# One loop that hands out every engine's steps in the recurrence stage of a decoder block, with r, k and v kept on chip and the inverses in zeroed double buffers

## The chip, the cores and the metric

The kernel runs on one core of one Trainium2 chip. The metric is device time in microseconds (us) of one execution; lower is better. The engines spoken of are PE (TensorE, matmuls), DVE (VectorE), ACT (ScalarE), POOL (GpSimd) and SP (SyncE, which here only issues DMAs). Each engine runs its own list of instructions in the order in which they stand; an instruction whose input is not there holds up all that stands behind it on that engine.

## The reference

One decoder block on 512 tokens of width 2048, all in float32. What the stage in question computes is the RWKV-7 mixer and the pooling mixer, both fed by one input projection:

```python
h = _rmsnorm(x, norm1_g[l]) * (1.0 + sc1) + sh1
p = h @ w_in[l]
y_rwkv = _rwkv7_mixer(p[..., :N_RWKV_COLS], ...)
y_pool = _pool_mixer(p[..., N_RWKV_COLS:], ...)
mix = jnp.concatenate([y_rwkv, y_pool], axis=-1) @ w_out[l]
x = x + gt1 * mix
...
def step(S, inp):                      # inside _rwkv7_mixer, per token and head
    r_t, w_t, k_t, v_t, a_t, b_t = inp
    sa = jnp.einsum('bhvk,bhk->bhv', S, a_t)
    S = S * w_t[:, :, None, :] + sa[..., None] * b_t[:, :, None, :] + v_t[..., None] * k_t[:, :, None, :]
    y = jnp.einsum('bhvk,bhk->bhv', S, r_t)
    return S, y
```

The shifts, scales and gates (`sh1` ... `gt2`) come from `mod = silu(c) @ w_ada + b_ada`, 12288 columns: a third is made in the opening, half in the stage in question (it is used after it), the rest later. After the mixers follow the output projection, a gated MLP with a short convolution, and a last norm.

## The kernel before, in words

The program has five parts that follow one another: an opening (norm, the first third of `mod`, the first eight 128-wide tiles of the input projection, L220-L232), the recurrence stage (this document's subject, L233-L755), the output projection, the MLP up and the MLP down. Every large matmul is done as three: weights and activations are split into a high and a low float32r part, and hi*hi, hi*lo and lo*hi are summed (`mm3`, L119-L124). The split of a weight block of 128x512 is a cast on ACT (L115, `whi`) and a subtraction on DVE (L117, `wlo`).

In the recurrence stage four kinds of work run beside one another.

- **Projection.** 27 tiles of 128 output columns each: r, k and v of pairs 1 to 7, then six pooling tiles. A tile is 48 matmuls of 128x512 (L333, `mm<-ah,whi` and so on) from four weight blocks: 1296 matmuls and 108 blocks. A finished tile is shifted by a token (`shift`: one ACT and one DVE instruction, L235 and L236). For the pairs the result goes to DRAM (`spill`, `sp`, L648) and is loaded again when the pair begins (`rkv`, `v`, L387).
- **Recurrence.** The 16 heads are taken as 8 pairs of 128 channels, the 512 tokens as 8 chunks of 64. Inside a chunk the token loop becomes matrix products and the inverse of a unit triangular 64x64 matrix, 16 of them for a pair. `stage_a` builds decays, normalised keys and the scores `sb` (L378, masked on DVE at L450). The 16x16 blocks on the diagonals are then inverted: eight DMAs take them to DRAM (`dn`, L456), one brings them back in another layout (`nl`, L458), 28 small DVE instructions do the substitution (`prod` and `xyl`, L472 and L474, between L466 and L475), one DMA writes the result (`dx`, L477), eight bring it back into place (`x4w`, L479; the rest of that tile was zeroed once), and ACT copies it to a second tile (L482). This document calls the way from the first `dn` DMA to that copy the trip. `stage_b` uses the inverses (first matmul L530, `pT`), widens them to 64x64 in two levels (L530 to L564), and carries the state over the chunks (L601 and L602 in turn, six times). `post` normalises and stores the pair (L619 to L636).
- **Pools.** Running sums on DVE (L285), and two products per group on PE (L300).
- **Rows of `mod`.** 192 loads of 256 KB (`war<-ada`, L350) into three buffers, each multiplied and summed by one DVE instruction (L351).

What sets the order: `recurrence` (L679) is a loop with one clock. Each piece of recurrence work ends in a `yield` of two numbers, the time that it takes on PE and the time before its successor may run; while no piece is ready, a projection matmul is handed out and counted as 0.23, and every sixth one brings a row of `mod`. PE keeps that order word for word (`manual_schedule`). DVE, ACT, POOL and SP do not: there the tool that builds the kernel sorts the instructions by a priority (`high_priority` for the recurrence) and by its own estimates of when each is ready. `q.inverted`, 44 units after the masks, sets where L530 stands on PE.

PSUM has eight banks of 128x512: the opening uses all eight as `pf0` to `pf7` from a pool of its own, and the stage's pool (`mm`, `pa`, `pb`, `py`) is opened when all `pf` have been read (L267 is the last).

Of the kernel before, what the change touches and what calls it, by code (L numbers as in the profile page):

```python
# [16 lines left out]
P = 128  # L17
T = 512
# [10 lines left out]
NB = 10  # L29
NJ = NF // 2  # L30
# [27 lines left out]
def block_kernel(ctx, tc, a, out, stop=None, dbg=None):  # L58
# [52 lines left out]
    def split_weights(src, eng=V):  # L111
        raw = wp.tile([P, WC], F32, tag="wraw", name="wraw", bufs=4)
        nc.sync.dma_start(raw, src)
        hi = wp.tile([P, WC], F32R, tag="whi", name="whi", bufs=3)
        S.copy(hi, raw)  # L115
        lo = wp.tile([P, WC], F32R, tag="wlo", name="wlo", bufs=3)
        eng.tensor_tensor(lo, raw, hi[:, :].bitcast(F32), op=ALU.subtract)  # L117
        return hi, lo
# [7 lines left out]
    def project(ps, src, acts, start=True, stop=True, engs=(V,)):  # L126

        n = len(acts)
        for k0 in range(0, n, WC // P):
            wh, wl = split_weights(src[:, k0 * P : k0 * P + WC], engs[k0 // 4 % len(engs)])  # L130
# [45 lines left out]
    first = {}  # L176
    p0ctx = ExitStack()
    p0 = p0ctx.enter_context(tc.tile_pool(name="p0", bufs=1))
    if True:
# [24 lines left out]
        ps0ctx = ExitStack()  # L204
        ps0 = ps0ctx.enter_context(tc.tile_pool(name="ps0", bufs=1, space=PSUM))
        pf = [ps0.tile([P, T], F32, tag=f"pf{i}", name=f"pf{i}") for i in range(8)]
        H = []
        for k in range(KT):
# [14 lines left out]
            for i0 in range(0, 8, WC // P):  # L223
                wh, wl = split_weights(a["win0"][k, :, i0 * P : i0 * P + WC])
                for ii in range(WC // P):
                    sl = slice(ii * P, (ii + 1) * P)
                    mm3(pf[i0 + ii], wh[:, sl], wl[:, sl], *H[k], start=k == 0, stop=k == KT - 1)
        p0ctx.close()


        actx = ExitStack()
        ra = actx.enter_context(tc.tile_pool(name="ra", bufs=1))  # L232
        if True:  # L233
            def shift(ps, m, dst):
                S.activation(dst, ps, AF.Copy, scale=drv[:, m : m + 1])  # L235
                V.scalar_tensor_tensor(dst[:, 1:T], ps[:, 0 : T - 1], col("mu", m), dst[:, 1:T],  # L236
                                       op0=ALU.mult, op1=ALU.add)

            def ring(name):
                return ring16(name)[:, 16:]  # L240

            def ring16(name):
                return ra.tile([P, 16 + T], F32, tag="ring", name=name, bufs=7)

            xwa = ra.tile([P, T], F32, tag="xwa", name="xwa")
            shift(pf[0], 24, xwa)
            S.activation(xwa[0:64, :], xwa[0:64, :], AF.Tanh)
            xg1 = ra.tile([P, T], F32, tag="xg1", name="xg1")
            shift(pf[1], 25, xg1)
            S.activation(xg1, xg1, AF.Sigmoid)  # L250
            xg2 = ra.tile([P, T], F32, tag="xg2", name="xg2")
            shift(pf[2], 26, xg2)
            S.activation(xg2, xg2, AF.Sigmoid)

            def vtile(name):
                return ra.tile([P, T], F32, tag="v", name=name, bufs=2)

            rkv0 = []
            for i, m in ((3, 0), (4, 8), (5, 16)):
                t = vtile("v") if i == 5 else ring("rkv")  # L260
                shift(pf[i], m, t)
                rkv0.append(t)

            upad = [ring16("upad") for i in range(2)]
            for i in range(2):
                V.memset(upad[i][:, 0:16], 0.0)
                S.copy(upad[i][:, 16:], pf[6 + i])  # L267
            ps0ctx.close()

    def load_pw(gi):  # L270
        t = ra.tile([P, T], F32, tag="war", name="pw", bufs=3)
        pw = t.rearrange("p (i d) -> p i d", i=2)
        nc.sync.dma_start(pw, a["poolw"][gi, :, :, :])
        return pw

    def pool_front(gi, upad):
        win = WINS[gi]
        zs = []
        for i in range(2):
            cur = upad[i]  # L280
            lo = 1
# [1060 lines left out]
```

## Time and profile before

| | us |
|---|---|
| median of 3 runs (2345.34 to 2349.33) | 2347.96 |
| the profiled execution, its own time | 2349.0 |
| its span, first to last instruction | 2347.1 |
| recurrence stage: end of the opening's last matmul to the first matmul of the output projection | 156.0 to 761.05 |

A group's row gives line, engine, operation, output and inputs, shapes and count, then busy time and the mean of one, then the engine's idle time just before these instructions and what ended it. "PE" is a matmul, "PEld" its weight load, "SPq" the issue of a DMA on SP's queue; a DMA lands some time after its issue. A row of a window gives busy us with the number of instructions for each engine, the granted PE clock (1.00 is full speed), the share of time in which the DMA engines worked, and GB/s. Ends of matmuls are modelled, so the distance from start to start is the better measure of what one costs in a stream.

### The profile page before, as it was taken

The page shows a single profiled execution, that of the slowest core. Times are in us where ns is not written, and L with a number is a line of the kernel's source. Part 1 is how long each engine was busy: PE and PEld are TensorE (multiplying, and loading weights), DVE is VectorE, ACT ScalarE, POOL GpSimd, SP SyncE. Part 2 cuts the span into 40 slices and gives each one's busy share as a digit, 9 for nine tenths or more (in the row PEclk, how much of TensorE's full clock was granted, in tenths as well). Part 3 has the DMA queues.
Part 4 walks back from the last instruction along what each step waited for, and adds up shares of the span by engine and source line. Part 5 has one row for each costly group of instructions (what it writes and reads, how often), then busy time and mean ns, then how long its engine had stood idle before and what let it go on. Part 6 is the DMA issues. An engine that isn't in the chain of part 4 may idle for free.

```text
span 2347.1 us, 42629 instructions
## 1 busy us (share of the span) xinstructions
PE 2206.0 (94%) x17090; PEld 1958.5 (83%) x17090; DVE 1611.8 (69%) x2543; ACT 1006.5 (43%) x1416; POOL 126.1 (5%) x183
## 2 busy tenths in 40 slices
PE   4778798898899999999999999999999999999997
PEld 3656566666677799999999999999999888888897
DVE  7977786877665366788888877777777645353454
ACT  3243333333333346655555555555555422233353
POOL 0000000000000010111010100000000000110000
PEclk9999899999999999999999999999999999999998
DMA  9966665666533766698888877777776667663464
GB/s 353 339 221 187 210 198 168 202 201 186 151 77 93 251 187 184 204 271 235 250 225 248 234 200 201 199 199 197 200 197 196 221 222 268 226 211 112 124 189 155
DMA packets 200218, 480.77 MB, mean 205 GB/s; under 512 B 46481, under 2 KB 53201, under 8 KB 191825
## 3 DMA queue, kind: packets, MB, share of 16 engines
q1 hardware_dynamic: 180098, 410.91, 53.7%
q0 software_dynamic: 18864, 66.07, 13.7%
q8 instruction: 134, 2.20, 0.4%
q10 hardware_dynamic: 1056, 1.05, 0.1%
q14 instruction: 66, 0.54, 0.1%
HBM read 440.45 MB, written 37.49 MB: 204 GB/s over the span
## 4 chain that ended last, share of the span: by engine, by line
PE 67%; DVE 12%; issue 11%; DMA 8%; ACT 2%; SPq 1%; POOL 0%; DVEq 0%; POOLq 0%; ACTq 0%
PE b L124 18%; PE b L122 18%; PE b L123 18%; PE mm L333 6%; DMA war<-ada 6%; DVE jk L214 3%; DVE war L351 2%; DVE wlo L117 1%; DMA wrow<-wup 1%; PE pa L300 1%; DVE sacc L199 0%; DVE al L151 0%; PE pb L570 0%; ACT ah L150 0%; DMA cq<-cact 0%
## 5 line engine op out<-in xcount | busy, mean ns | idle before, releaser
L124 PE MATMUL b<-t,ulo 128*128 128x256 f32 x1408 | 397.2, 282 | 0.0
L122 PE MATMUL b<-t,uhi 128*128 128x256 f32 x1408 | 396.8, 282 | 0.0
L123 PE MATMUL b<-t,uhi 128*128 128x256 f32 x1408 | 396.7, 282 | 0.0
L115 ACT CAST whi<-wraw 128x512 fp32r<-128x512 f32 x236 | 145.4, 618 | 381.9 <-PE mm L333 222.9
L124 PE MATMUL b<-act,ulo 128*128 128x512 f32 (+1 forms) x880 | 308.0, 350 | 0.0
L123 PE MATMUL b<-act,uhi 128*128 128x512 f32 (+1 forms) x880 | 307.8, 350 | 0.0
L122 PE MATMUL b<-act,uhi 128*128 128x512 f32 (+1 forms) x880 | 307.7, 350 | 0.0
L122 PE MATMUL b<-y,uhi 128*128 128x256 f32 x1056 | 298.1, 282 | 2.1 <-ACT uhi L930 2.1
L124 PE MATMUL b<-y,ulo 128*128 128x256 f32 x1056 | 297.8, 282 | 0.4 <-DVE ulo L932 0.4
L123 PE MATMUL b<-y,uhi 128*128 128x256 f32 x1056 | 297.9, 282 | 0.0
L932 DVE TENSOR_TENSOR ulo<-wd,uhi 128x1024 fp32r<-128x1024 f32 (+1 forms) x120 | 136.2, 1135 | 215.6 <-ACT uhi L930 210.8
L122 PEld LDWEIGHTS b<-t,uhi 128*128 128x128 f32 x1408 | 266.9, 190 | 0.0
L124 PEld LDWEIGHTS b<-t,ulo 128*128 128x128 f32 x1408 | 266.9, 190 | 0.0
L123 PEld LDWEIGHTS b<-t,uhi 128*128 128x128 f32 x1408 | 266.8, 190 | 0.0
L930 ACT CAST uhi<-wquart 128x1024 fp32r<-128x1024 f32 x156 | 163.8, 1050 | 203.8 <-PE b L123 177.5
L930 ACT CAST uhi<-wd 128x1024 fp32r<-128x1024 f32 (+1 forms) x120 | 117.3, 978 | 291.1 <-PE b L123 290.0
L932 DVE TENSOR_TENSOR ulo<-wquart,uhi 128x1024 fp32r<-128x1024 f32 x156 | 190.9, 1224 | 71.9 <-ACT uhi L930 71.9
L117 DVE TENSOR_TENSOR wlo<-wraw,whi 128x512 fp32r<-128x512 f32 x236 | 161.2, 686 | 82.3 <-ACT whi L115 81.5
L930 ACT CAST uhi<-r 128x1024 fp32r<-128x1024 f32 x132 | 138.6, 1050 | 162.8 <-PE b L123 159.2
L932 DVE TENSOR_TENSOR ulo<-r,uhi 128x1024 fp32r<-128x1024 f32 x132 | 161.2, 1222 | 61.8 <-ACT uhi L930 61.7
L122 PEld LDWEIGHTS b<-y,uhi 128*128 128x128 f32 x1056 | 200.2, 190 | 2.5 <-ACT uhi L930 2.5
L124 PEld LDWEIGHTS b<-y,ulo 128*128 128x128 f32 x1056 | 200.1, 190 | 0.6 <-DVE ulo L932 0.6
(302 smaller groups left out, 4455.7 us busy)
## 6 DMA issues: line engine op xcount, KB each, us to landing
wquart<-wup SPq DMA_DIRECT2D x176, 512.0 KB, 4.8
wa<-ada SPq DMA_DIRECT2D x48, 1024.0 KB, 6.9
war<-ada SPq DMA_DIRECT2D x192, 256.0 KB, 3.6
wd<-wdn SPq DMA_DIRECT2D x80, 512.0 KB, 4.0
wraw<-win SPq DMA_DIRECT2D x140, 256.0 KB, 4.2
wraw<-wout SPq DMA_DIRECT2D x96, 256.0 KB, 3.6
wquart<-wup POOLq DMA_DIRECT2D x44, 512.0 KB, 7.3
r<-wup SPq DMA_DIRECT2D x44, 512.0 KB, 4.5
```

Of the source, the lines that this page charges most:

```text
L115: S.copy(hi, raw)
L117: eng.tensor_tensor(lo, raw, hi[:, :].bitcast(F32), op=ALU.subtract)
L122: PE.matmul(ps, wh, xh, start=start, stop=False, skip_group_check=more)
L123: PE.matmul(ps, wh, xl, start=False, stop=False, skip_group_check=more)
L124: return PE.matmul(ps, wl, xh, start=False, stop=stop, skip_group_check=more)
L214: V.scalar_tensor_tensor(jk, wa, 1.0, cb, op0=ALU.mult, op1=ALU.mult, accum_out=mod[:, j : j + 1])
L300: PE.matmul(ps, pw[:, i, d * P : (d + 1) * P], zs[i], start=i == 0, stop=i == 1)
L333: PE.matmul(ps, w[:, sl], x, start=k == 0 and i == 0, stop=k == KT - 1 and i == 2)
L351: V.scalar_tensor_tensor(wa, wa, 1.0, cq[0], op0=ALU.mult, op1=ALU.mult, accum_out=modq[:, kq, j : j + 1])
L930: S.copy(hi[:, 0:n], src)
L932: lo_of[0] = V.tensor_tensor(lo[:, 0:n], src, hi[:, 0:n].bitcast(F32), op=ALU.subtract)
```

## The change

What it does, by parts:

- **One loop for all engines.** Every step of every chain of work is a generator that yields an engine ("P", "V", "S", "Q" for SP, "-" for a mere condition), the time that the step holds it, and the time (or a function that gives it) before which it cannot run. `run` keeps a clock per engine, takes the step that can start earliest, lets one of better priority go ahead if it starts little later, and then emits it. The order of PE, DVE, ACT, POOL and SP is that of emission (`manual_schedule()` without a list of engines). Priorities: opening and evictions 0, `stage_b` 1, `stage_a` and `post` 2, `stage_k` (the part of `stage_a` that the inverses do not need) 3, weight blocks 0 to 4 by how near PE is to needing them, pools 5, projection matmuls 6, rows of `mod` 7.
- **r, k, v on chip.** `evict` shifts a tile into one of three `rk` or two `v` buffers, which `stage_a` reads; the 21 stores to DRAM and 21 loads are gone.
- **Inverses.** `x4` is two whole tiles, zeroed by POOL for every pair, into which the `dx` DMAs write; the ACT copy L482 is gone. `gd`, `sg` and two `fdec` tiles are zeroed once by POOL, where DVE wrote `sg`'s and `fdec`'s edges for every pair.
- **Rows of `mod`.** Five buffers in place of three, four loads ahead, each row due 460/192 units after the one before.
- **PSUM.** The opening uses the stage's own banks, and a bank is free when its own tile has been read.
- **Weights.** The first two blocks of the stage are loaded before the opening's pool is closed, later ones two blocks ahead.
- **Small ones.** Several tiles have one buffer instead of two, or share one (`sq`, `inv`; `y`, `sqy`, `rs`); a pool's result overwrites its input by way of a 16-wide `edge` tile, one more small DVE copy each; the gate product of `post` stands earlier on PE.

```diff
+NA = 4
+WARB = 5
+NTILE = 27
+PF0 = 5.5
+SPAN = 460.0
+ADAB = 0.72
...
-        ps0ctx = ExitStack()
-        ps0 = ps0ctx.enter_context(tc.tile_pool(name="ps0", bufs=1, space=PSUM))
-        pf = [ps0.tile([P, T], F32, tag=f"pf{i}", name=f"pf{i}") for i in range(8)]
+        psctx = ExitStack()
+        psa = psctx.enter_context(tc.tile_pool(name="psa", bufs=1, space=PSUM))
+        pf = [psa.tile([P, T], F32, tag=t, name="pf") for t in ("mm0", "mm1", "pa0", "pa1")]
+        for t in ("pb", "py"):
+            two = psa.tile([P, 2, T], F32, tag=t, name="pf")
+            pf += [two[:, 0, :], two[:, 1, :]]
...
+    LAT = {"P": 0.3, "V": 0.2, "S": 0.2, "Q": 0.0}
...
+    def run():
+
+        while chains:
+            best = {}
+            for c in chains:
+                eng, busy, after = c[2]
+                t = after() if callable(after) else after
+                if t is None:
+                    continue
+                t = max(t, free_at.get(eng, 0.0))
+                best.setdefault(eng, []).append((t, c[0]() if callable(c[0]) else c[0], busy, c))
+            pick = None
+            for eng, ops in best.items():
+                op = min(ops, key=lambda o: o[:2])
+                late = [o for o in ops if o[1] < op[1] and o[0] < op[0] + min(0.3, 0.5 * op[2])]
+                if late:
+                    op = min(late, key=lambda o: o[1])
+                if pick is None or op[:2] < pick[:2]:
+                    pick = op
+            t, _, busy, c = pick
+            eng = c[2][0]
+            if eng in free_at:
+                free_at[eng] = t + busy
+                t += busy + LAT[eng]
+            try:
+                c[2] = c[1].send(t)
+            except StopIteration:
+                chains.remove(c)
...
+    def weights():
+
+        land = {0: 0.5, 1: 1.0}
+        for i in range(4 * NTILE):
+            wnext[0] = i
+            if i + 2 < 4 * NTILE and i + 2 not in land:
+                t = yield "Q", 0.35, 0.0
+                load_block(i + 2)
+                land[i + 2] = t + 3.8
+            t = yield "S", 0.58, (lambda i=i: land[i] if i <= cur[0] + 2 else None)
+            raw = blocks.pop(0)
+            hi = wp.tile([P, WC], F32R, tag="whi", name="whi", bufs=3)
+            S.copy(hi, raw)
+            t = yield "V", 0.63, t
...
+    def evict(ti, ps, tag, t):
+        if ti < 21:
+            p, i = ti // 3 + 1, ti % 3
+            q = qs[p]
+            dst = vtile("v") if i == 2 else rktile("rk")
+            t = yield "S", 0.6, t
+            shift1(ps, 8 * i + p, dst)
+            t = yield "V", 0.65, t
+            shift2(ps, 8 * i + p, dst)
+            mm.give(tag, t)
...
+    def ada_rows():
+        n_all = 48 * NA
+        step = SPAN / n_all
...
+        for n in range(n_all):
+            kq, j = divmod(n, 48)
+            t = yield "V", ADAB, max(land[n], tcq, 3.0 + n * step)
+            wa = was.pop(0)
+            V.scalar_tensor_tensor(wa, wa, 1.0, cqs[kq], op0=ALU.mult, op1=ALU.mult, accum_out=modq[:, kq, j : j + 1])
...
+            if n + WARB - 1 < n_all:
+                tq = yield "Q", 0.35, 0.0
+                load_ada(n + WARB - 1)
+                land[n + WARB - 1] = tq + 4.5
...
-        x4 = q.x4 = ra.tile([P, 8, 2, 64], F32, tag="x4c", name="x4")
-        S.copy(x4, x4w)
-        q.inverted = clock[0] + 44.0
-        yield 1.35, 6.0
...
+        x4 = q.x4 = ra.tile([P, 8, 2, 64], F32, tag="x4", name="x4", bufs=2)
+        G.memset(x4, 0.0)
...
+            t = yield "Q", 0.33, t
+            nc.sync.dma_start(x4[16 * b : 16 * b + 16, :, :, 16 * (b % 4) : 16 * (b % 4) + 16],
+                              dx[8 * b : 8 * b + 8, :, :, :].rearrange("s w i j -> i s w j"))
+        q.inverted = t + 2.4
...
+    with tc.manual_schedule():
+        for prio, gen in ((0, opening()), (1, all_b()), (2, all_a()), (weights_prio, weights()), (6, projection()), (7, ada_rows())):
+            spawn(prio, gen)
+        run()
```

Every later stage keeps its instructions, on DVE, ACT and POOL in the same order as before; what moves lies in the recurrence stage. Three places show how. In the rows below a line number is that of the kernel the row belongs to: L550 after is L351 before (a row of `mod`), L416 is L117 (`wlo`), L638 is L450 (the masks on the scores), L654 is L466 and L666 is L475 (first and last step of the substitution), L661 and L663 are L472 and L474.

On DVE before, the fifth pair's masks and its substitution:

```order
L351 SCALAR_TENSOR_TENSOR war,modq<-war,cq 128x512 x2
L573 COPY rw<-pb 128x512
L351 SCALAR_TENSOR_TENSOR war,modq<-war,cq 128x512
L450 TENSOR_TENSOR sb<-pa,masks 128x4x128 x2
...
L466 TENSOR_TENSOR xyl<-nl,lanei 64x256
L602 SCALAR_TENSOR_TENSOR rw<-pb,fdec,rw 128x64
L472 TENSOR_TENSOR prod<-xyl,nl 64x14
L117 TENSOR_TENSOR wlo<-wraw,whi 128x512
L474 TENSOR_TENSOR xyl<-xyl,prod 64x14
L351 SCALAR_TENSOR_TENSOR war,modq<-war,cq 128x512
L472 TENSOR_TENSOR prod<-xyl,nl 64x26
```

On DVE after, the same pair:

```order
L686 TENSOR_TENSOR kt<-rk,em 128x512
L884 TENSOR_TENSOR y<-y,bv 128x512
L638 TENSOR_TENSOR sb<-pa,masks 128x4x128 x2
L726 TENSOR_TENSOR sk<-pb,masks 128x1024
...
L550 SCALAR_TENSOR_TENSOR war,modq<-war,cq 128x512
L654 TENSOR_TENSOR xyl<-nl,lanei 64x256
L661 TENSOR_TENSOR prod<-xyl,nl 64x14
L663 TENSOR_TENSOR xyl<-xyl,prod 64x14
L661 TENSOR_TENSOR prod<-xyl,nl 64x26
```

Before, rows of `mod` stand ahead of the masks and other work stands between nearly every two steps of the substitution; after, no row of `mod` stands near the masks, and all 28 steps from L654 to L666 stand one behind the other (in the second pair one other instruction is among them).

On SP after, the fifth pair's trip and what is queued between its DMAs (`x` is the tile that the inverses go to):

```order
L647 DMA dn_4153<-sb 16x8x16 x8
L889 DMA mixd_103<-y 128x512
L119 DMA wraw<-win 128x512
L532 DMA war<-ada 128x512
L119 DMA wraw<-win 128x512
L532 DMA war<-ada 128x512
L651 DMA nl<-dn_4153 64x256
...
L669 DMA dx_4364<-xyl 64x512
L353 DMA lw<-lora 128x128
L119 DMA wraw<-win 128x512 x2
L532 DMA war<-ada 128x512 x2
L673 DMA x_4151<-dx_4364 16x16x16 x8
```

Weight blocks and rows of `mod` now stand at fixed places between the trip's DMAs; the stores and loads of `sp` that stood there before are gone. On PE the first matmul that needs the inverses (L771, before L530) stands behind 80 projection matmuls counted from the end of that pair's scores in the first pair, 54 in the second, 88, 72, 87, 72, 80 and 87 in the others, with recurrence work of its own and of the neighbouring pair among them.

More of the change, by code (lines that the diff above doesn't have):

```diff
@@ L227, in block_kernel @@
                     mm3(pf[i0 + ii], wh[:, sl], wl[:, sl], *H[k], start=k == 0, stop=k == KT - 1)
+        for i in range(2):
+            load_block(i)
         p0ctx.close()
[L231 to L268, printed above, removed]
@@ L537, in stage_b @@
[L537 removed]
+        pa.give(tag, t)
+        t = yield "P", 1.9, max(t, tpb)
         pX = btile()
@@ L734, in block_kernel, with all_a, all_b @@
[L734 to L740 removed]
+    def all_a():
+        for p in range(NP):
+            yield from stage_a(p, qs[p])
+    def all_b():
+        for p in range(NP):
+            yield from stage_b(p, qs[p])
+    G.memset(gd, 0.0)
+    G.memset(sg, 0.0)
```

697 lines of the change are left out of this document (410 added, 287 removed).

## The prediction

> **What bounds the kernel now.** I read the page first, for the stage that the change touches, then windows, the waits, and the timeline at the longest waits. Of the page, four rows of the span in 40 slices (58.7 us each) and the chain of waits:
>
> ```profile
> PE   4778798898899999999999999999999999999997
> DVE  7977786877665366788888877777777645353454
> PEclk9999899999999999999999999999999999999998
> DMA  9966665666533766698888877777776667663464
> PE 67%; DVE 12%; issue 11%; DMA 8%; ACT 2%; SPq 1%; POOL 0%; DVEq 0%; POOLq 0%; ACTq 0%
> ```
>
> From the 14th slice on PE works nine tenths of the time or more: those parts are bound by PE, and none of them changes. The recurrence stage is slices 3 to 13, where PE has gaps and DVE is at 6 to 8 tenths. In windows (opening's end, stage with rows of `mod`, stage without them, whole stage):
>
> ```profile
> 156.00:163.09 7.09, 0.04 (x2) 0.00 (x1) 4.48 (x11) 7.00 (x12) 0.00 (x0) 0.76 0.32 110
> 163.09:650.00 486.91, 427.06 (x4251) 319.74 (x4252) 362.58 (x959) 172.52 (x265) 0.00 (x0) 0.94 0.62 187
> 650.00:761.00 111.00, 110.05 (x1231) 84.40 (x1230) 61.98 (x139) 32.83 (x54) 0.00 (x0) 1.00 0.31 86
> 156.00:761.05 605.05, 537.19 (x5481) 404.16 (x5481) 429.05 (x1107) 212.37 (x332) 0.00 (x0) 0.95 0.56 168
> ```
>
> The stage takes 605.05 us. PE is idle for 67.9 of them, and its clock is 0.95; at 650, when the last row of `mod` is done, idle time and low clock both end. So the stage is bound by PE, which is held up while the rows of `mod` run. Who holds it up, in the waits of PE:
>
> ```profile
> PE pb L563 <- DVE Tm L560: 15.4, 4, 6.5
> PE pb L601 <- DVE rw L602: 9.6, 10, 1.7
> PE mm L333 <- DVE wlo L117: 8.1, 3, 4.7
> PE pa L426 <- ACT sq L395: 8.0, 1, 8.0
> PE mm L333 <- ACT upad L267: 7.1, 1, 7.1
> ```
>
> And why DVE is late (group of L351, two waits, two rows of the timeline):
>
> ```profile
> L351 DVE SCALAR_TENSOR_TENSOR war<-war,cq 128x512 f32<-128x512 f32 x192 | 129.8, 686 | 84.0 <-DMA war<-ada 76.7 <-DMA cq<-cact 6.7
> DVE wlo L117 <- ACT whi L115: 18.3, 19, 2.2
> DVE rw L573 <- ACT rw L573: 15.7, 6, 4.3
> 543.18 0.69 DVE L351 SCALAR_TENSOR_TENSOR war<-war,cq 128x512 f32<-128x512 f32 x1 [3.68 <-DMA war<-ada]
> 543.79 1.28 DVE L450 TENSOR_TENSOR sb<-pa,masks 128x512 f32<-128x512 f32 x2
> ```
>
> DVE stands idle 84.0 us ahead of rows of `mod` whose load has not landed, and what PE needs (here the masks L450, at other places `Tm` L560) is queued behind them.
>
> **How much work PE has.** Between the first use of the inverses of the last two pairs lies nearly one pair's work without waits; the window once for all of PE, once for L333 alone, then the pace of L333 (13 issues, 12 distances) and one pool product:
>
> ```profile
> 650.45:704.70 54.25, 53.30 (x639) 40.66 (x638) 33.21 (x86) 15.91 (x26) 0.00 (x0) 1.00 0.31 78
> 650.45:704.70 54.25, 32.57 (x117) 1.00 0.31 78
> 645.29 0.39 PE L333 MATMUL mm<-al,whi 128*128 128x512 f32 x1
> ...
> 648.01 0.39 PE L333 MATMUL mm<-al,whi 128*128 128x512 f32 x1
> 698.12 3.59 PE L300 MATMUL pa<-z,pw 128*128 128x512 f32 x8
> ```
>
> The distance is 2.72 / 12 = 0.227. Off 54.25 go 117 x 0.227 = 26.5, the idle 0.95 and the pool's 3.4: 23.4 for the pair; its L401, L402 and L426 fell outside. They are six passes 512 wide, 2.6 at the pool's 3.4 / 8 each, or 1.7 if L401 and L402, which use half of the rows each, run side by side; I take 2.2. That is 25.6 a pair. The stage: 1296 x 0.227 = 294, 8 x 25.6 = 205, three pool products 10: **509 us**. Busy time by clock says the same: 537.19 x 0.95 = 510.
>
> **The change part by part.**
>
> *PSUM banks and early weights.* The first projection matmul waits 7.1 us for L267, the reader of the last opening bank. After, it needs only the bank of the first tile, which is read while the opening's last matmuls run, and a weight block that is loaded by then. Gain between 5 and 7.1; it is inside the 605 - 509.
>
> *Rows of `mod`.* 192 stay. With five buffers a load is issued four rows ahead; a row comes every 509/192 = 2.65 us, so it has 10.6 us to land, against
>
> ```profile
> DMA to landing us min/median/max: 2.4/3.6/6.5
> ```
>
> So the 84.0 of idle DVE ahead of them goes, unless SP is held up. DVE's work, 429 us, has 530 to fit in.
>
> *The trip.* Here a new wait may take the place of the old. Before, L530 stands so late in PE's order that it hardly waits. After, the order leaves fixed cover. From the end of a pair's scores to L771 PE has 54 to 88 projection matmuls and recurrence work; in the fifth pair that is 87 x 0.227 = 19.7 and second scores, four transposes, L692, L750, L758 and L762, an estimated quarter of the pair's 25.6, 6.3: 26.0 us, and, worked out alike, 26 to 27 in all others but the first (80 matmuls, a pool product and more: 29). What must fit in, from the fifth pair (rows of `mod` running) and the last (done), first `dn`, L466, L475, then `x4w`, L482:
>
> ```profile
> 470.45 4.45 SPq L456 DMA_DIRECT2D dn<-sb  x8
> 479.92 0.42 DVE L466 TENSOR_TENSOR xyl<-nl,lanei 64x256 f32<-64x256 f32 x1
> 499.30 0.38 DVE L475 COPY xyl<-xyl 64x256 f32<-64x256 f32 x1
> 509.26 1.05 ACT L482 COPY x<-x4w 128x1024 f32<-128x1024 f32 x1 [1.90 <-DMA x4w<-dx]
> ...
> 662.23 1.29 DVE L450 TENSOR_TENSOR sb<-pa,masks 128x512 f32<-128x512 f32 x2 [2.84 <-PE pa L378]
> 663.55 4.54 SPq L456 DMA_DIRECT2D dn<-sb  x8
> 672.08 0.41 DVE L466 TENSOR_TENSOR xyl<-nl,lanei 64x256 f32<-64x256 f32 x1
> 677.98 0.21 DVE L472 TENSOR_TENSOR prod<-xyl,nl 64x56 f32<-64x56 f32 x1
> 678.22 0.21 DVE L474 TENSOR_TENSOR xyl<-xyl,prod 64x56 f32<-64x56 f32 x1
> 682.72 0.37 DVE L475 COPY xyl<-xyl 64x256 f32<-64x256 f32 x1
> 686.00 3.77 SPq L479 DMA_DIRECT2D x4w<-dx  x8
> 692.69 1.05 ACT L482 COPY x<-x4w 128x1024 f32<-128x1024 f32 x1
> ```
>
> The trip took 38.8 us in the fifth pair and 29.1 in the last; the substitution alone 19.4 and 10.6. Unbroken, its 28 steps take at most 0.24 each (677.98 to 678.22) and L466 0.41: 7.1. The rest was 9.5 + 10.0 in the fifth pair and 8.5 + 10.0 in the last. So the trip becomes 25.6 to 26.6; the copy of 1.05 after it is gone. The masks ahead of it take 1.29 and a start of some 0.2. Need 27.1 to 28.1, cover 26.0: PE waits 1.1 to 2.1 in seven pairs, nothing in the first. I take 1.5: **10.5 us**; ends 0 (the DMAs may land before ACT was free to look) and 15.
>
> *The clock after such waits.* The same product warm, after 2.17 and after 4.24 us of waiting:
>
> ```profile
> 665.09 1.15 PE L563 MATMUL pb<-x,Tm 64*64 64x64 f32 x32
> 531.49 1.82 PE L563 MATMUL pb<-x,Tm 64*64 64x64 f32 x32 [2.17 <-DVE Tm L560]
> 272.90 1.97 PE L563 MATMUL pb<-x,Tm 64*64 64x64 f32 x32 [4.24 <-DVE Tm L560]
> ```
>
> A wait of two microseconds already costs 0.7 to 0.8 on the next product. Seven waits at half of it: **3 us**, ends 0 and 6. [...]
>
> *Handovers inside `stage_b`.* The 9.6 and 15.4 us of waits at L601 and L563 came with DVE's queue; the steps that follow one another are now spaced by projection matmuls. Some remain, since rows of `mod` still stand between steps of DVE (three between L793 and L798 in the fifth pair). Ends 0 and 25 (all that these two lines show); I take **8**, nearer to zero as in the stretch from 650.
>
> *r, k, v on chip.* 42 DMAs of 256 KB go, 11 MB of the stage's 605 us x 168 GB/s = 102 MB; the DMA engines work 0.56 of the time, so nothing is gained by that alone, and if the cover fails nothing is lost. Two shift instructions per tile stay. The price is that a new tile waits for its buffer's last reader, with ACT's weight casts queued behind it; in the order those readers stand ahead of the shift on every engine: 0.
>
> *SP.* The eight `x4w` issues wait for `dx` to land; behind them stand weight blocks and rows of `mod`, loaded two and four ahead. Hidden by those; if not, a block late costs what L117 cost PE before, 8.1 in all.
>
> *POOL and small DVE edits.* Eight more memsets on an engine that the four windows show idle; one 0.15 us copy more for each pool tile, some memsets fewer: 0, under the other terms' error.
>
> *After the stage* the order on DVE, ACT and POOL is unchanged and PE has work without gaps, so the gain carries to the end.
>
> **Sum.** 509 + 10.5 + 3 + 8 = 530.5 in place of 605.05: 74.5 saved. The profiled execution took 2349.0, 1.0 over the median: 2274.5, and against the median **2273**.
>
> **The rivals.**
>
> *Better than that:* no waits and all of PE's work at full clock, 509: 96 saved, 2252. For it: 650 to 761 ran almost so. Against: the cover of 26.0 is about equal to the shortest trip.
>
> *VectorE becomes the bound.* 429.05 of work, and if it still waits as before, 84.0 + 18.3 + 15.7: 547 us, 58 saved, 2290. For it: 81% of the new stage is its work, in a fixed order. Against: five buffers.
>
> *The trip shortens by half only,* say to 33, because SP, now in a fixed order, issues its seventeen DMAs late. Need 34.5, cover 26: 8.5 x 8 = 68, and 6 for the clock: 591, 14 saved, 2334.
>
> *Slower:* the trip stays at 38.8 (DMAs land late beside denser loads). PE's cover is fixed, so it waits 38.8 + 1.5 - 26 = 14.3 in eight pairs, 114, with 6 for the clock and 8 of handovers: 637, 32 more, 2380. It decides from a trip of about 35 on, where 8 waits of 10.5 with those 14 eat the 96. Against: more than half of the trip's length was interrupted substitution, and that is settled by the order.
>
> *The change doesn't do what it says:* PE's order was already full and the time stays. Against: 67.9 idle and 0.95 clock.
>
> **How the numbers follow.** My forecast 0.60; better 0.06; VectorE 0.12; half a trip 0.12; slower 0.08; no change 0.02. Faster by over 0.2% (4.7 us, about what a measurement of this kernel tells from nothing) 0.90, within 0.02, slower 0.08. The range runs from 2248 (some below the better case, if a pair's work is nearer 25) to 2330, the edge of the half trip; it leaves out the slower case and part of that one.
>
> **What would show it.** After: the stage from 156 to about 687; PE idle about 20 in it, clock at 0.98 or above; L771 waiting for `x` some 10 us in all and L796 and L844 little; no wait of 84 at rows of `mod`; from first `dn` to L771 about 26. A clock still at 0.95, or L771 above 50, would make the prediction wrong.

## The result, and the profile after

| | before | after |
|---|---|---|
| median, us | 2347.49 (2345.34 to 2349.33) | 2307.67 (2304.52 to 2314.75) |
| the profiled execution | 2349.0 | 2314.75 |
| first projection matmul to the first of the output projection | 163.1 to 761.05 | 155.2 to 721.75 |

The ratio is 0.9835, with a 95% interval of 0.9809 to 0.9860: 39.8 us faster by the medians, where 74.5 were forecast. Sign and range held; the size was about half. The profiled execution of the changed kernel is the slowest of its four, which comes up again below.

The stage in one row of the windows for each kernel, before and after, from the first to the last projection matmul (PE busy, PE weight loads, DVE, ACT, POOL, then granted clock, DMA share, GB/s):

```profile
163.10:760.40 597.30, 536.50 (x5478) 403.61 (x5479) 424.56 (x1097) 205.34 (x319) 0.00 (x0) 0.95 0.57 168
155.20:721.10 565.90, 533.05 (x5479) 401.94 (x5478) 441.77 (x1100) 204.14 (x321) 5.72 (x6) 0.97 0.55 160
```

After the change it is 565.9 us, 533.05 busy and so 32.85 idle. To see what the clock takes, I cut the stage into 23 equal slices and sum busy time x (1 - clock): 15.5 us. What is left, 517.5, is PE's work at full clock. By the same accounting the stage before is 597.3 = 60.8 idle + 23.3 clock + 513.3 work. So 27.9 of idle and 7.8 of clock went, the opening's wait of 7 went, and 4.2 of busy time came on top.

The waits of the changed kernel in the stage (total us, times, longest):

```profile
DVE war L550 <- DMA war<-ada: 22.8, 21, 4.4
...
PE pa L771 <- DMA x<-dx: 12.8, 9, 2.1
...
DVE Tm L774 <- PE pa L771: 10.9, 4, 3.8
...
PE mm L440 <- DVE wlo L416: 7.8, 3, 3.6
DVE xyl L654 <- DMA nl<-dn: 7.3, 4, 3.3
```

(L771 is the first product that uses the inverses, L774 the masking of its result on VectorE, L781 the two products that need that; L440 is a projection matmul, L416 makes its `wlo`.) VectorE's wait for rows of `mod` to land fell from 76.7 (the 84.0 of before hold 6.7 for `cq` too) to 22.8 but did not go. PE's longest item is L771, as forecast. One of these, in the fourth pair, on PE's timeline:

```profile
388.08 0.39 PE L440 MATMUL mm<-ah,wlo 128*128 128x512 f32 x1
390.60 0.29 PE L771 MATMUL pa<-x,sb 64*64 64x64 f32 x2 [2.13 <-DMA x<-dx]
392.07 1.94 PE L771 MATMUL pa<-x,sb 64*64 64x64 f32 x30 [1.17 <-DMA x<-dx]
393.94 0.79 PE L440 MATMUL mm<-ah,whi 128*128 128x512 f32 x1
394.53 0.63 PE L440 MATMUL mm<-al,whi 128*128 128x512 f32 x1
...
396.37 1.97 PE L781 MATMUL pb<-Tm,x 64*64 64x64 f32 x32
398.13 1.17 PE L781 MATMUL pb<-x,Tm 64*64 64x64 f32 x32
```

PE waits for the first `x` DMA, does two matmuls, waits for the others, and then everything takes nearly twice its time until about 398: the projection matmuls stand 0.43 apart at 394.5 to 395.8 where 0.227 is the full clock, the first product of L781 takes 1.97 and the second 1.17. That is how 3.3 us of waiting cost seven. The same with the granted clock, at another wait:

```profile
211.00:213.00 2.00, 0.04 (x1) 0.00 (x0) 1.95 (x6) 0.00 (x0) 0.00 (x0) 1.00 0.93 317
213.00:213.50 0.50, 0.41 (x14) 0.41 (x16) 0.50 (x2) 0.00 (x0) 0.00 (x0) 1.00 0.80 209
213.50:217.00 3.50, 3.50 (x60) 3.23 (x57) 2.37 (x4) 1.67 (x3) 0.00 (x0) 0.56 0.39 120
217.50:221.00 3.50, 3.50 (x42) 2.40 (x41) 2.55 (x6) 1.26 (x2) 0.00 (x0) 1.00 0.45 123
```

Two idle microseconds at full clock, half a microsecond of work, and then a stretch of about 3.5 us at half. In windows of half a microsecond the stage has eight such stretches, six of about 3.5 and two of 7 us, each behind a wait or a close pair of waits that make 1.6 to 3.6 us: five behind L771, one behind L781 (the rows above), two behind L440.

One of the two at L440, on VectorE and then on PE:

```profile
445.83 0.42 DVE L654 TENSOR_TENSOR xyl<-nl,lanei 64x256 f32<-64x256 f32 x1 [1.35 <-DMA nl<-dn]
...
452.64 0.37 DVE L666 COPY xyl<-xyl 64x256 f32<-64x256 f32 x1
452.94 1.88 DVE L416 TENSOR_TENSOR wlo<-wraw,whi 128x512 fp32r<-128x512 f32 x3
```

```profile
453.67 0.79 PE L440 MATMUL mm<-ah,wlo 128*128 128x512 f32 x1 [3.15 <-DVE wlo L416]
```

Three `wlo` stand behind the unbroken substitution, which itself had waited for `nl`.

### The profile page after: what moved, and what is told of

Read it like the earlier page. It is cut to its first block, busy times and chain, and to the rows that moved or that the text cites. A ratio compares the mean times of both kernels' runs of the same rounds, so it can differ in the third digit from the quotient of the medians.

```text
span 2313.0 us, 42595 instructions
## 1 busy us (share of the span) xinstructions
PE 2205.9 (95%) x17090; PEld 1959.5 (85%) x17090; DVE 1625.4 (70%) x2535; ACT 998.9 (43%) x1406; POOL 133.3 (6%) x193
## 4 chain that ended last, share of the span: by engine, by line
PE 84%; DVE 7%; DMA 4%; ACT 2%; issue 1%; SPq 0%; DVEq 0%; ACTq 0%
PE b L133 21%; PE b L131 21%; PE b L132 21%; PE mm L440 10%; DVE jk L231 3%; DMA war<-ada 2%; DMA wrow<-wup 1%; PE pb L781 1%; DMA nl<-dn 1%; PE pb L804 1%; PE pa L504 1%; DVE prod L661 0%; DVE xyl L663 0%; DVE sacc L213 0%; PE pa L738 0%
## 5 line engine op out<-in xcount | busy, mean ns | idle before, releaser
L1110 ACT CAST uhi<-wquart 128x1024 fp32r<-128x1024 f32 x156 | 163.8, 1050 | 204.1 <-PE b L132 175.8
L1110 ACT CAST uhi<-wd 128x1024 fp32r<-128x1024 f32 (+1 forms) x120 | 117.4, 978 | 291.8 <-PE b L132 291.6
L1110 ACT CAST uhi<-r 128x1024 fp32r<-128x1024 f32 x132 | 138.6, 1050 | 163.0 <-PE b L132 161.5
L131 PEld LDWEIGHTS b<-y,uhi 128*128 128x128 f32 x1056 | 200.3, 190 | 5.2 <-ACT uhi L1110 5.2
L132 PEld LDWEIGHTS b<-y,uhi 128*128 128x128 f32 x1056 | 199.9, 189 | 0.0
L440 PE MATMUL mm<-ah,wlo 128*128 128x512 f32 x432 | 181.7, 421 | 8.0 <-DVE wlo L416 7.8
```

What stands on the lines that cost most here:

```text
L131: PE.matmul(ps, wh, xh, start=start, stop=False, skip_group_check=more)
L132: PE.matmul(ps, wh, xl, start=False, stop=False, skip_group_check=more)
L440: PE.matmul(ps, w[:, sl], x, start=first, stop=k == KT - 1 and i == 2)
L1110: S.copy(hi[:, 0:n], src)
```

## The experiments

All runs are edits of the changed kernel. The table gives the stage from first to last projection matmul of each profiled execution, split as above, and the ratio to the kernel before on the same chip. The experiments ran on four chips, so they are best compared by their ratios.

| run | stage | idle | clock | ratio (95%) |
|---|---|---|---|---|
| the changed kernel | 565.9 | 32.9 | 15.5 | 0.9835 (0.9809 to 0.9860) |
| the same again | 562.7 | 32.0 | 13.9 | 0.9823 (0.9797 to 0.9849) |
| e1 inverses later | 550.9 | 29.6 | 3.3 | 0.9797 (0.9773 to 0.9821) |
| e2 no rows | 529.3 | 12.6 | 0 | 0.9689 (0.9669 to 0.9710) |
| e3 no trip | 524.6 | 9.5 | 0 | 0.9666 (0.9646 to 0.9687) |
| e4 three buffers | 559.4 | 32.3 | 7.6 | 0.9870 (0.9854 to 0.9886) |
| e5 rows on POOL | 570.0 | 36.2 | 18.2 | 0.9857 (0.9830 to 0.9885) |
| e6 trip priced | 519.7 | 6.0 | 0 | 0.9785 (0.9756 to 0.9814) |
| e7 rows later | 552.3 | 24.5 | 10.7 | 0.9838 (0.9812 to 0.9865) |
| e8 both | 521.2 | 6.8 | 0 | 0.9905 (0.9880 to 0.9931) |
| e9 all priced | 533.7 | 15.3 | 0 | 0.9775 (0.9755 to 0.9795) |
| e10 rows sooner | 540.1 | 23.1 | 0 | 0.9765 (0.9748 to 0.9783) |
| e11 rows spread | 533.6 | 15.6 | 0 | 0.9754 (0.9737 to 0.9770) |

PE's work at full clock is 514 to 520 in all of them: what differs is idle time, clock, and what happens behind the stage.

**e1: only L771 later.**

```diff
-        q.inverted = t + 2.4
+        q.inverted = t + 6.4
```

> The changed kernel with one number altered: q.inverted is 6.4 in place of 2.4 units after the last of the x4 DMAs, so L771 is handed out four units later on PE and projection matmuls stand in the gap. Theory (short waits and the clock behind them): the changed kernel waits 12.8 us at L771 in nine places, and nearly every stretch with a clock of 0.93 or less lies right behind one of them; by busy time x (1 - clock) those stretches lose 15.5 us. With L771 later both go: the stage falls from 567 to about 543 us and the time from 2307.7 to about 2285. Rival (VectorE sets the pace, and L771 is only where it shows): the wait comes back at L781, L796, L804 or at a wlo, the stage gains less than 5 us: 2303 to 2308. Second rival (the clock falls anyway): only the 12.8 us go: 2295.

Measured 2301.07. L771's wait went, and a wait at the next step took its place:

```profile
PE pb L781 <- DVE Tm L774: 17.4, 8, 4.0
```

The longest, on VectorE and then on PE:

```profile
582.12 0.69 DVE L550 SCALAR_TENSOR_TENSOR war<-war,cq 128x512 f32<-128x512 f32 x1 [4.71 <-DMA war<-ada]
...
584.75 0.69 DVE L774 TENSOR_TENSOR Tm<-pa,mlev 128x512 f32<-128x512 f32 x1
```

```profile
585.49 1.50 PE L781 MATMUL pb<-Tm,x 64*64 64x64 f32 x32 [4.02 <-DVE Tm L774]
```

`Tm`, the 0.69 us step between two products of PE, stands on VectorE behind a row of `mod` that had not landed. So the first rival was right on where the wait went. It was wrong that nothing would be gained: idle time is nearly the same (29.6 for 32.9), and yet the profiled stage is 15 us shorter, because the clock takes 3.3 in place of 15.5. (The medians are only 6.6 us apart and the intervals of the ratios overlap, so the gain in time is not clear of the noise.) Here the clock is nearly all that differs. Why is less plain, since e1 has waits as long. This one, of 2.21 us at L781, left the clock alone:

```profile
261.50:264.00 2.50, 0.43 (x14) 0.43 (x16) 2.49 (x6) 0.28 (x1) 0.00 (x0) 1.00 1.05 387
264.00:267.50 3.50, 3.50 (x66) 3.12 (x61) 3.16 (x9) 0.00 (x0) 0.00 (x0) 1.00 0.97 318
```

Behind e1's longest wait, the 4.02 us above, the first product of L781 took 1.50 us; behind the 2.21 us it took 1.15.

Windows set at the falls and rises of the clock show the stretches more sharply. In the profiled execution of the changed kernel they start at 213.95, 258.32, 333.42, 391.44, 452.88, 524.56, 589.41 and 650.85; six last 3.41 us and two, at 391.44 and 452.88, 6.83, all at 0.50. The first of them:

```profile
213.95:217.36 3.41, 3.41 (x45) 3.10 (x42) 2.27 (x5) 1.67 (x3) 0.00 (x0) 0.50 0.27 74
```

PE had waited 2.04 us (from 211.04) ahead of this one, and 1.64 us (at L771, from 255.39) ahead of the second; e1's 2.21 us is longer than either and left the clock at 1.00. So the length of one wait does not decide by itself whether half clock follows, and the runs do not show what does. Ends of matmuls are modelled, so these lengths are not sharp.

**e2 and e3: one of two loads taken away.** Both keep every other instruction in its place. e2 emits no loads and products of rows of `mod` (one memset on POOL zeroes the sums in their place); e3 emits nothing of the trip, from the `dn` DMAs to the `x4` DMAs, so `x4` stays zero.

```diff
-            load_ada(n)
...
-            V.scalar_tensor_tensor(wa, wa, 1.0, cqs[kq], op0=ALU.mult, op1=ALU.mult, accum_out=modq[:, kq, j : j + 1])
...
-                load_ada(n + WARB - 1)
```

and for e3

```diff
-            nc.sync.dma_start(dn[8 * b : 8 * b + 8, :, :].rearrange("s i j -> i s j"),
...
-            V.tensor_tensor(pv, xyl[:, 1, 0:s, s : s + 1].to_broadcast([64, s, n]),
...
-            nc.sync.dma_start(x4[16 * b : 16 * b + 16, :, :, 16 * (b % 4) : 16 * (b % 4) + 16],
```

> The changed kernel with the 192 rows of mod left out of the stage: neither their loads (L532) nor their products (L550) are emitted, the sums are zeroed instead; every other instruction keeps its place, since the steps are still counted in the order. So 128 us of VectorE's 442 us of work, 50 MB of DMA and the 22.8 us of waits at L550 go. Theory (short waits of PE and the clock): these waits reach PE only through a late nl or wlo, so idle falls from 33 to about 20 us and the cold stretches by a third: stage about 550, time about 2290. Rival (VectorE sets the pace): the stage goes to PE's own 518 us, time about 2260. Second rival (rows are wholly beside the path): within 4 us of 2307.7.

> The changed kernel with the trip left out: no dn, nl, dx and x DMAs and no substitution; x4 keeps POOL's zeros, so the inverses are missing from the result; every other instruction keeps its place, the steps being still counted in the order. L771 can then wait only for nt and the zeros. Theory: the 12.8 us at L771, the two waits of 3.6 and 3.2 us at L440 behind the substitution, and the cold stretches behind them (most of 15.5 us) go: stage about 535, time about 2277; PE's busy time at full clock stays at 518. Rival (the missing gain is PE's own work, sized at 509, or other handovers): only the 20 us of waits go, the clock stays at 0.97: 2288 or more. What the stage still takes over 518 is the price of all handovers that are not the trip's.

Measured 2275.37 and 2269.62. The stage of each:

```profile
154.50:683.80 529.30, 516.71 (x5479) 391.16 (x5477) 326.31 (x712) 204.65 (x321) 5.71 (x6) 1.00 0.30 76
```

```profile
156.70:681.30 524.60, 515.13 (x5479) 390.31 (x5478) 393.12 (x860) 203.99 (x320) 5.71 (x6) 1.00 0.55 166
```

Of 48.4 us of idle and clock together 12.6 and 9.5 are left, and the stages are 36.6 and 41.3 shorter. The two gains add up to more than the 48.4, so it is the two loads together that cost: the trip nearly fits under PE's cover when no rows are loaded beside it, and rows cost little when no trip runs (VectorE waits 6.9 for them in e3, 22.8 in the changed kernel). In e2 the trip is shorter though nothing of it was edited: from the first `dn` to the end of the last `x4` issue 22.1 to 25.5 us, 24.4 to 27.3 with rows, and L771 waits 2.0. The theory's 550 and 2290 for e2 were far off, and the rival's 518 and 2260 too low; e3 gained more than its theory's 535 and 2277. Rows reach PE through more than `nl` and `wlo`, namely through the trip's length and through `Tm`.

**e4: three buffers.**

```diff
-WARB = 5
+WARB = 3
```

> The changed kernel with three buffers for the rows of mod, as before the change, and so loads two ahead in place of four. By the forecast the five buffers took away the 84 us that VectorE waited for rows. Theory: with two loads ahead and 5.8 us from issue to landing, rows that stand in groups on VectorE wait again, some 40 to 80 us in all, and VectorE's later steps reach PE late: stage 580 to 600, time 2320 to 2340. Rival (the fixed order, not the buffers, took the waits away, since the rows are due at fixed times 2.4 units apart): waits at L550 stay under 40 us and the time within 5 us of 2307.7.

Measured 2318.28, below the theory's range and 10.6 above the rival's 2307.7, so neither held as to the time. The idle time of VectorE ahead of the rows:

```profile
  DMA war<-ada: 45.5, 48
```

Of the 76.7 us of before, the change with three buffers takes away 31.2 and the two more buffers another 22.7. The loss isn't in the stage (559.4): the last row stands at 751.3 in place of 713.9, in the output projection, and from the last projection matmul to the end of the span it takes 1605.1 in place of 1591.9.

**e5: rows on another queue.**

```diff
-        nc.sync.dma_start(t, a["ada2"][n // 48, n % 48, :, :])
+        nc.gpsimd.dma_start(t, a["ada2"][n // 48, n % 48, :, :])
```

> The changed kernel with the 192 loads of rows of mod (L532) issued by POOL in place of SP; nothing else moves. Leaving the rows out gave 2275, leaving the trip out 2270, the changed kernel 2308: it is the two together that cost. Theory (SP's queue): the trip's DMAs that wait for data hold up the row loads behind them, and the row loads take issue time between the trip's DMAs. On two queues both go: waits at L550 fall from 22.8 to under 10 us, the first x4 issue comes 2.4 us after dx in place of 3.0 to 4.5, L771 waits under 5 us, time about 2285. Rival (the DMA engines are shared: the trip's small packets land late beside 256 KB loads, whatever the queue): from dx to the first x4 stays at 3 us or more, L771 still waits 10 us or more, 2300 to 2312. Third (POOL is slow at issuing): rows land later than now, waits at L550 over 40 us, slower than 2315.

Measured 2313.51: no gain. From the groups of DMA issues (count, KB each, median us to landing) of the changed kernel and of e5, and then PE's wait at L771 and VectorE's for rows in e5:

```profile
x<-dx SPq DMA_DIRECT2D x64, 16.0 KB, 2.8
```

```profile
x<-dx SPq DMA_DIRECT2D x64, 16.0 KB, 4.7
```

```profile
PE pa L771 <- DMA x<-dx: 17.9, 8, 4.4
```

```profile
DVE war L550 <- DMA war<-ada: 9.6, 13, 1.6
```

The queue did hold things up: rows wait 9.6 in place of 22.8, and from the `dx` issue to the first `x4` issue it is 2.3 us in seven pairs (2.9 to 4.5 in seven pairs of the changed kernel). But the `x4` DMAs land in 4.7 us in place of 2.8, and L771 waits longer. So the theory is wrong as to the time. The first rival (shared DMA engines) comes nearest (L771 waits over 10 us, and the time is 1.5 above its range), though its sign that the `x4` issues stay late did not come: freed of the queue, the small DMAs land later beside the rows. Whether that is the sharing of the DMA engines or something in POOL's way of issuing, the run doesn't tell.

**e6, e7, e8: the loop's prices.** The loop places steps by the times it is told. e6 tells it the trip's true ones (in the order of the lines: `dn`, `nl`, a step of the substitution, `x4`), e7 a longer landing of rows, e8 both.

```diff
-            tn = yield "Q", 0.33, tn
+            tn = yield "Q", 0.45, tn
-        t = yield "V", 0.4, t + 3.6
+        t = yield "V", 0.42, t + 5.0
-            t = yield "V", 0.36, t
+            t = yield "V", 0.46, t
-            t = yield "Q", 0.33, t
+            t = yield "Q", 0.6, t
```

and the row's landing:

```diff
-                land[n + WARB - 1] = tq + 4.5
+                land[n + WARB - 1] = tq + 8.0
```

> The changed kernel with the trip's steps priced in the loop as the trace has them: a dn issue 0.45 (was 0.33), nl 5.0 after its issue (3.6), a step of the substitution 0.46 (0.36), an x4 issue 0.6 (0.33). The order then has L771 about 6 units later, and Tm, the wlo behind the substitution and the row loads on SP stand where they come out in truth. Theory: unlike the run that only moved L771 (2301, the wait came back at L781 for Tm), the steps behind move with it: L771 and L781 together wait under 10 us, no wlo wait over 1 us, cold under 5 us, time about 2292. Rival (row loads late on SP still hold Tm): L781 waits 15 us again, 2298 to 2303.

> The changed kernel with the landing of a row of mod priced at 8.0 units after its issue in place of 4.5 (the trace has 5.8 from issue to landing as the median, and SP holds some issues up), so its product stands later on VectorE. Theory (rows that have not landed stand ahead of the steps PE waits for): waits at L550 fall from 22.8 to about 8 us; L771 still waits about 10 us, since its own DMAs are as late: 2300. Rival (waits at L550 are not what holds PE): within 4 us of 2308.

> Both tables of prices together: the trip's as in the run with the trip priced, the row's landing at 8.0. Theory: the two waits that feed each other (L771 on the trip, Tm behind rows that have not landed) go together, PE idle under 18 us, cold under 3 us, stage about 540, time about 2283. Rival (moving both later only pushes the pair's later steps into the end of the stage, where no projection is left): 2298 or more.

Measured 2296.22, 2310.11 and 2324.44. e6's stage, then its largest wait of PE, and SP's row behind that:

```profile
155.00:674.70 519.70, 513.74 (x5478) 390.53 (x5477) 419.65 (x1035) 201.53 (x316) 5.72 (x6) 1.00 0.54 158
```

```profile
PE pb L131 <- ACT whi L124: 26.9, 1, 26.9
```

```profile
669.62 25.59 SPq L532 DMA_DIRECT2D war<-ada  x28
```

The stage is shorter than the prediction's 530.5: 519.7 with 6.0 idle and no clock lost. So PE's waits in the stage came from the prices. But it is not the same work in less time, because the rows are not through: 26 of the 192 products stand behind the stage's last projection matmul, 28 loads are issued in one run from 669.6 on, as PE finishes the projection, and the output projection's first weights stand behind them. By the profiles 46 us were gained in the stage and 26.9 paid back at once; by the ratios the kernel gained about 12 us over the changed kernel, and the two intervals overlap a little. e8 shows it larger:

```profile
PE pb L131 <- ACT whi L124: 53.4, 2, 37.1
```

```profile
690.39 38.49 SPq L532 DMA_DIRECT2D war<-ada  x43
```

I had not expected this in e8 at all: as I read it, pricing a row's landing at 8 with five buffers slows the rows, and 56 products are left when the projection ends; no run takes that apart. e8's rival had 2298 or more, but for another reason. e7 falls to the same (a wait of 9.8 there) and its L771 still waits 11.4: no gain, as its rival said, though its waits at L550 did fall, to 3.7. (The expectations of e4 and e7 give 5.8 us from a row's issue to its landing; the trace of the changed kernel has 4.2 as the median.)

**e9, e10, the changed kernel again: rows priced as measured.**

On top of e6, with 3.3 in place of 3.85 in e10:

```diff
-ADAB = 0.72
+ADAB = 0.62
...
-                land[n + WARB - 1] = tq + 4.5
+                land[n + WARB - 1] = tq + 3.85
```

> The kernel with the trip priced, and the rows of mod priced as measured as well: a product 0.62 (was 0.72), a landing 4.2 after its issue, so 3.85 after the step (was 4.5). With the trip priced alone PE's projection ended 519.7 us after its first matmul with 6.0 us idle and no cold stretch, but 31 rows were left over, SP issued 28 of them in a run from 669.6 to 695.3, and PE then waited 26.9 us for the first weights of the output projection, which stand behind them. Theory: in the loop's own clock the last row moves from 531 to 510 and the last projection tile from 516 to 511, so that wait falls to under 3 us; the stage takes 520 to 530 us and the time is 2268 to 2278, ahead of both kernels. Rival (rows packed more densely bring the waits back): idle of 20 us or more in the stage, 2290 or more.

> The same with a landing priced at 3.3 after the step, less than measured: rows stand a little sooner on VectorE, last row at 507 by the loop's clock. Theory: the wait ahead of the output projection is gone as well, but rows that have not landed stand ahead of the steps PE waits for: waits at L550 back to 20 us or more, L781 or L771 waiting 5 to 10 us; 2275 to 2285. Rival (with the trip priced there is slack enough on VectorE): equal to the run before it within 4 us.

> The changed kernel unaltered, beside the two others on the same chip: 2304 to 2315, ratio 0.981 to 0.986. If its executions differ again by 10 us, the clock in them differs too: a shorter one has a higher mean clock, since a wait of about two microseconds at L771 sometimes brings a cold stretch of 3.5 us and sometimes not.

Measured 2295.41, 2292.71 and 2305.33. The wait ahead of the output projection in e9, and in e10:

```profile
PE pb L131 <- ACT whi L124: 13.4, 1, 13.4
```

```profile
PE pb L131 <- ACT whi L124: 4.4, 1, 4.4
```

It shrinks as rows come sooner, and the stage grows: 519.7 in e6, 533.7, 540.1. Stage and wait together are 546.6, 547.1 and 544.5: time moved from one place to the other. Both theories missed, since they counted the wait as gone for nothing. Both rivals had the time (2290 or more for e9; within 4 us of e9 for e10) but not the reason: e9 idles 15.3 in the stage, not 20, and e10 idles 7.8 more than e9, so VectorE had no slack left. The changed kernel again ran from 2300.58 to 2311.69, at a mean clock of 0.990 and 0.985.

**e11: the last 16 rows between the blocks of the output projection.**

On top of e9; `more_rows` is the product of L550 with the next load issued by POOL:

```diff
+NROW = 176
...
-        for n in range(n_all):
+        for n in range(NROW):
...
         last = out_block(f, 0)
+        more_rows(NROW + 2 * f, NROW + 2 * f + 2)
```

> The kernel with the trip and the rows priced as measured, with the last 16 of the 192 rows of mod taken out of the stage's loop and handed out two at a time between the first eight blocks of the output projection, their loads issued by POOL; the sum over rows follows them. Theory (what is left over is the rows' own time on VectorE and SP, which the stage cannot hide when PE goes through it in 520 to 535 us): the wait of 13.4 us ahead of the output projection and the 17.5 us at half clock behind it, worth 8.7, go; VectorE is idle more than half of the time there and hides the 16 rows: 2295.4 - 13 to 22 = 2272 to 2282. Rival (the output projection's own weights are split on VectorE and now wait behind rows): the wait only moves by 20 us and the time stays at 2290 to 2297.

Measured 2287.43, the lowest of the kernels that do all the work, and its interval is clear of both of the changed kernel's, as e9's and e10's are; it overlaps with theirs. The wait (one line lower in this kernel's text) went from 13.4 to 5.1. That is 8 us, as much as lies between the medians of e9 and e11; by the ratios it is 5:

```profile
PE pb L132 <- ACT whi L125: 5.1, 1, 5.1
```

The theory asked for 13 to 22. It counted half of the 17.5 us at half clock as lost, but PE was busy for only 6.2 of them, and by busy time x (1 - clock) 3.0 us are lost there.

## Why the prediction was right or wrong

The four terms of the stage's sum, forecast and measured in the profiled execution: work 509 and 517.5; waits at L771 10.5 and 12.8; clock 3 and 15.5; handovers 8, and 20.1 for all idle time but L771's. Together 530.5 and 565.9. The excess of 35.4 is 8.5 + 2.3 + 12.5 + 12.1. The direction was right; the size was not, and the time lies in the range because the range was wide. Of the signs that were named beforehand, the clock (0.97 in place of 0.98) and the idle time (32.9 in place of about 20) missed; L771 and the wait for rows, far from 84, held.

- **Opening: right.** The first projection matmul stands at 155.2, was 163.1.
- **PE's work: 8.5 too low.** The windows of before give 513.3 by slices; the instruction counts at best durations gave 509. The other 4.2 came with the change, and from what is open.
- **The trip and L771: right in the sum, in part by luck.** The substitution took 6.8 us in seven pairs (7.1 forecast). But from the first `dn` to L654 it was 8.7 to 13.0 (8.5 to 9.5 forecast), and the last `x` DMA landed 25.9 to 29.0 us after the first `dn`, where the forecast has the trip end after 25.6 to 26.6. L771 waited in five pairs, 1.6 to 3.4 us in each, where 1.5 in seven was forecast. In two of the three others, the fifth and the eighth, PE had lost 3.15 and 3.59 us at L440 on the way, behind the same pair's substitution.
- **The clock after such waits: the step that failed most,** 3 forecast, 15.5 measured and above its end of 6. I priced a wait by its effect on the next product alone (0.7 to 0.8). What follows is a stretch of 3.41 or 6.83 us at half clock, up to 1.7 or 3.4 lost each time by busy time x (1 - clock); the one at 213.95 followed a single wait of 2.04 us, the one at 258.32 a wait of 1.64. What sets a stretch off the runs do not show.
- **Handovers: about right for what the term meant.** It was for the steps inside `stage_b`. L781, L816, L844, L804, L750 and L790 wait 6.6 us together, 8.9 with L701's wait for `kt`; forecast 8. The rest of the 20.1 is other idle time, most of it L440 waiting 7.8 for `wlo`, which stands behind the substitution on VectorE, begun late for `nl`: a wait I took at nothing, though the forecast itself made the substitution one unbroken block. The prediction's paragraph on SP has a price for a late block, 8.1, but lets it hang on SP and not on this.
- **Rows of `mod`: "the 84 goes" was wrong;** 22.8 stayed, and through the trip and `Tm` they are one of the two roots of the idle time and the clock: without rows (e2) these are 12.6 together in place of 48.4, and without the trip (e3) 9.5.
- **SP at nothing:** not settled. SP's order did delay rows and trip (e5), but moving the rows to POOL's queue gained nothing, because the `x` DMAs then landed later (4.7 us in place of 2.8); no run shows what SP's order costs by itself.
- **After the stage** the profiled execution took 5.2 us more than before (1591.3 to the end of the span, 1586.1), 2.5 of it at L1110's `uhi` (4.6, was 2.1 at L930); the rest I have not traced.
- **r, k, v on chip** was not run by itself; its price of nothing is untested. Which part of the change brought the 39.8 us is not taken apart either: the earlier first projection matmul is 7.9 of them, and e4 puts the two more buffers at about 8 by the ratios (the intervals overlap a little).

Of the rivals, VectorE as the bound (2290) named the right engine and the wrong mechanism. VectorE's queue is not full (441.8 of 565.9), but the rows must pass through it and through SP beside the trip, and when PE goes through in 520 they are left over. That PE's order was already full before is refuted by the gain. Whether the stage with all its rows can take 530.5 is open: stage and the wait behind it make 545 to 547 in e6, e9 and e10, and 538.7 in e11, which does 16 rows later.

The median is 7 us below the profiled execution. Over executions of the same kernel time and mean clock go together (2304.52 at 0.990, 2314.75 at 0.985); that this is the number of half-clock stretches is likely from the sums above (eight in one trace of the changed kernel, seven in the other), but only one execution of each run has a trace.

## What to carry to other kernels

Where a loop places the steps of all engines by a table of durations, the waits that are left may lie where a duration in the table is too short: compare the table with the trace, chain by chain, before looking for a deeper limit (e6: four numbers took PE's idle time in the stage from 32.9 to 6.0 us). Ask of work "beside the path" not only whether it fits but where its rest stands in the queue when the path gets shorter; here 28 late loads paid back 27 of the 46 us that e6 had gained in the stage. And price a wait of two microseconds on PE with the clock that may follow it, not with its own length alone (behind the 2.04 us at 211 stood 3.41 us at clock 0.50).

## What the runs showed of the hardware

In the recurrence stage the granted clock fell to 0.50 for 3.41 or 6.83 us at a time in the changed kernel, and for 3.41, 6.83 and once 10.24 us (at 234.75) in the kernel before. Each of the eight stretches of the changed kernel came with a wait of PE, or a close pair of waits, of 1.64 to 3.59 us. A wait of 2.21 us in e1 (to 263.57) left the clock at 1.00, waits of 2.04 us (to 213.09) and 1.64 us (to 257.03) in the changed kernel did not, and the stages of e6, e9, e10 and e11, with longest single waits of 1.3 to 2.5 us, had no stretch. What decides is open. DMAs of 16 KB beside loads of 256 KB: the `x` DMAs landed in 2.3 us as the median without rows (e2), in 2.8 with rows on the same queue, and in 4.7 with rows on a second queue (e5).
